# A mixture-of-experts loop: the planner's order against an order written out by hand

## The chip, the cores and the metric

The kernel runs on one core of one Trainium2 chip. The metric is the device time of one execution in microseconds (us), the median of several runs. The kernel is one launch; it moves 524 MB between the chip's main memory and the core's SBUF.

## The reference

A bidirectional encoder of two layers over 1024 tokens and 16 leading meta tokens, D = 1024. Each layer has an attention and a recurrent (RWKV-7) group of heads, an output projection and a LayerNorm, and then the part that this case is about, a mixture of 32 experts of which each token takes two:

```
def expert_block(args):
    xe, e = args
    return (jax.nn.silu(xe @ w1[e]) * (xe @ w3[e])) @ w2[e]
...
y = jnp.zeros((T, D)).at[row_tok].add(yb * row_gate[:, None])
...
h = _layer_norm(DN_ALPHA * h + ff, ln2_g[li], ln2_b[li])
```

w1 and w3 of an expert are 1024x256, w2 is 256x1024, so an expert has 3 MB of float32 weights, and a layer 96 MB. The 2080 choices of layer 0 (2048 of layer 1) spread over the experts, about 65 tokens each.

## The kernel before

`moe_layer` computes the experts one after the other with room for 96 tokens each (CAP); what is over goes through a general path, `tc.If(n_over > 0)`, that these inputs do not take. Products are float32 made from two parts: each operand is split into a high part (rounded to fp32r) and a low part (the remainder), and `mm3` issues three matmuls, high by high, high by low, low by high.

Per expert these steps run. A gather by row numbers (L1259, an indirect DMA issued on POOL) brings the tokens to `xs` (two buffers, one for even and one for odd experts). `turned` (L1229) transposes them on TensorE in two halves into the two PSUM buffers `tp`; ACT copies each half as high part `xT_hi` (L209), DVE subtracts to get `xT_lo` (L212). The weights come in three thirds of 1 MB, [128, 2048] each, by DMAs on the SP queue (L1211) into six buffers `raw`, so that two experts' weights fit; ACT makes the high part in four pieces (`w_hi`, L1216), and the low part is made by DVE in four pieces for the first two thirds, and by POOL in two pieces for the last third (`w_lo`, L1220). Six pairs of buffers hold the split thirds. 24 matmuls make the hidden layer `ph` (L201 to L203) from the first two thirds, one third for each half of `xT`. ACT takes tanh (L1239), DVE two instructions for the gated unit (L1240, L1241), TensorE transposes the result through `tp` (L1244), ACT and DVE split it (`aT`). 12 matmuls with the last third make `py`; ACT scales the left half to `y` (L1253), DVE the right half (L1254), and an indirect DMA on POOL scatters the rows to `y_rows` (L1255).

The program text has these steps expert by expert. The order on each engine's queue is set by the framework's planner, which runs a timing model over the whole program and takes what it expects to be ready; `tc.issue_after` pins only the first experts' splits behind the router. At run time each engine takes its queue in order and waits with semaphores. A buffer pool hands a new tile one of its free buffers, and the tile's first writer waits until the last reader of that buffer is done.

After the loop the check for the general path follows: six small DVE instructions on the counts (L1291 to L1299), a load of the result into a register of every engine (L1300), and a branch on every engine (L1302). Then `combine` (L334 to L354) takes both rows of each token from `y_rows` (`ys`), adds them on POOL (L344), forms `ALPHA * x + sum` with its row total on DVE (L346), and does the LayerNorm: a square with sum on ACT (L224), a power on POOL (L226), two passes on DVE (L227, L228). After layer 0 it transposes the rows for the next layer's projection; after layer 1 it stores the output. It works on 9 tiles of tokens after layer 0, on 8 after layer 1.

Of the kernel before, what the change touches and what calls it, by code (L numbers as in the profile page):

```python
# [11 lines left out]
F32 = mybir.dt.float32  # L12
# [22 lines left out]
NE = 32  # L35
# [135 lines left out]
def hybrid_encoder(ctx: ExitStack, tc: tile.TileContext, I, out):  # L171
# [141 lines left out]
    def combine(li, hT, pp):  # L313

        end = li == DEPTH - 1
        with ExitStack() as st:
# [20 lines left out]
            for i, n, col in tiles:  # L337
# [842 lines left out]
def moe_layer(tc, I, li, last, K, split, mm3, stack, rt, route, h1_rows, y_rows, nt, dram):  # L1180
# [18 lines left out]
    with pool(tc, name="mop", bufs=1, space=PSUM) as pp:  # L1199
# [5 lines left out]
        def weights(src, spaces=(ra, rc, rb), late=True):  # L1205

            r = []
            for q in range(3):
                raw = spaces[thirds[0] // 2 % len(spaces)].tile([128, 2048], F32, name="raw")
                thirds[0] += 1  # L1210
                nc.sync.dma_start(raw, src(q))  # L1211
                w = pair(ww, [128, 2048], "w")

                for c in range(4):
                    cs = slice(c * 512, (c + 1) * 512)
                    nc.scalar.activation(w.hi[:, cs], raw[:, cs], AF.Copy)  # L1216
# [4 lines left out]
                r.append(w)  # L1221
            return r

        def turned(x, n):
            xT = pair(wx, [128, 8, 128], "xT")[:, :, :n]
            for q in range(2):
                tp = pp.tile([128, 4, 128], F32, name="tp", bufs=2)
                for c in range(4):
                    nc.tensor.transpose(tp[:, c, :n], x[:n, (4 * q + c) * 128:(4 * q + c + 1) * 128], ident[:n, :n])  # L1229
                xT.last = split(xT[:, 4 * q:4 * q + 4], tp[:, :, :n])  # L1230
            return xT

        def expert(w, xT, n, vs, gs, rows):
            ph = pp.tile([128, 512], F32, name="ph", bufs=2)
            for kc in range(8):
                mm3(ph[:n], xT[:, kc], w[kc // 4][:, kc % 4 * 512:(kc % 4 + 1) * 512], start=kc == 0, stop=kc == 7)
# [4 lines left out]
            V.scalar_tensor_tensor(th, th, 0.5, ph[:n, 256:], op0=OP.mult, op1=OP.mult)  # L1241
            tp = pp.tile([128, 4, 128], F32, name="tp", bufs=2)
# [3 lines left out]
            split(aT, tp[:, 0:2, :n])  # L1246
            py = pp.tile([128, D], F32, name="py", bufs=2)
            for j in range(2):
                for c in range(2):
                    mm3(py[:n, j * 512:(j + 1) * 512], aT[:, c], w[2][:, c * D + j * 512:c * D + (j + 1) * 512],  # L1250
                        start=c == 0, stop=c == 1)
            y = wk.tile([128, D], F32, name="y")
            nc.scalar.activation(y[:n, :512], py[:n, :512], AF.Copy, scale=gs)  # L1253
            V.tensor_scalar(y[:n, 512:], py[:n, 512:], gs, None, op0=OP.mult)  # L1254
# [8 lines left out]
        def of(e, late=True):  # L1263
            return weights(lambda q: I["w_moe"][li, e, :, q * 2048:(q + 1) * 2048], late=late)

        def tokens(e):
            ins = gather(xs[e % 2][:CAP], h1_rows, XS[:CAP, e:e + 1], n_rows)
            return turned(xs[e % 2], CAP), ins
# [3 lines left out]


        (x0, _), (x1, second) = tokens(0), tokens(1)
        with tc.issue_after(route.act.ins), tc.issue_after(route.dve.ins), tc.issue_after(second.ins):
            ws = [of(0)]
        with tc.issue_after(x0.last[0].ins), tc.issue_after(x0.last[1].ins), tc.issue_after(second.ins):
            ws.append(of(1))
        xTs = [x0, x1]
        for e in range(NE):  # L1280
            if e + 1 < NE and e:
                ws.append(of(e + 1))
                xTs.append(tokens(e + 1)[0])
            expert(ws.pop(0), xTs.pop(0), CAP, VS[:CAP, e:e + 1], GS[:CAP, e:e + 1], views[e])


        tab = dram.tile([OVER * 128, 1], I32, name="ov_tab", tag="ov_tab", bufs=2)
        bex = dram.tile([1, OVER], I32, name="ov_bex", tag="ov_bex", bufs=2)
        gd = dram.tile([2 * n_rows, 1], F32, name=f"ov_gd{li}")
        nb = ov.tile([128, 4, NE], F32, name="nbs")  # L1290
        V.tensor_scalar(nb[:, 0], cnt, float(-CAP), 0.0, op0=OP.add, op1=OP.max)  # L1291
        ni = ov.tile([128, NE], I32, name="nis")
        V.tensor_scalar(ni, nb[:, 0], 127.0, None, op0=OP.add)
        V.tensor_scalar(ni, ni, 7, None, op0=OP.logical_shift_right)
        V.tensor_copy(nb[:, 0], ni)
        n1 = ov.tile([1, 1], F32, name="n1")
        V.tensor_reduce(n1, nb[0:1, 0], op=OP.add, axis=AX.X)
        nbi = ov.tile([1, 1], I32, name="nbi")
        V.tensor_copy(nbi, n1)  # L1299
        n_over = nc.values_load(nbi[0:1, 0:1], min_val=0, max_val=OVER,  # L1300
                                skip_runtime_bounds_check_because="2080 choices fill at most 21 such blocks")
        with tc.If(n_over > 0):  # L1302
            ini = ov.tile([128, OVER], I32, name="ini")
            V.tensor_copy(ini, bc(K("slot"), [128, OVER]))
            nc.sync.dma_start(tab.rearrange("(p b) o -> p (b o)", p=128), ini)
            for q, i in enumerate(route.order):
                n = META if i == NT else 128
                nc.sync.dma_start(gd[256 * i:256 * i + 2 * n].rearrange("(p j) o -> p j o", j=2), route.gates[:n, :, q, None])
            nc.gpsimd.memset(nb[:, 3], 1.0)
            V.tensor_tensor_scan(nb[:, 1], nb[:, 3], nb[:, 0], 0.0, op0=OP.mult, op1=OP.add)  # L1310
            V.tensor_tensor(nb[:, 2], nb[:, 1], nb[:, 0], op=OP.subtract)

            bx = ov.tile([1, OVER, NE], F32, name="bx")
            V.tensor_tensor(bx, bc(nb[0:1, 1:2, :], [1, OVER, NE]),
                            bc(K("iota32")[0:1, :OVER, None], [1, OVER, NE]), op=OP.is_le)
            bi = ov.tile([1, OVER], F32, name="bi")
            V.tensor_reduce(bi[:, :, None], bx, op=OP.add, axis=AX.X)
            V.tensor_scalar(bi, bi, float(NE - 1), None, op0=OP.min)
            bii = ov.tile([1, OVER], I32, name="bii")
            V.tensor_copy(bii, bi)  # L1320
            nc.sync.dma_start(bex[:], bii)
            tm = ov.tile([128, nt, NE], F32, name="otm")
            pos = ov.tile([128, nt], F32, name="pos")
            big = ov.tile([128, nt], F32, name="big")
            for j in range(2):
                V.tensor_tensor(tm, M[:, j], bc(nb[:, 2:3, :], [128, nt, NE]), op=OP.mult)
                V.tensor_reduce(pos, tm, op=OP.add, axis=AX.X)
                V.scalar_tensor_tensor(pos, pos, 128.0, rk[:, j], op0=OP.mult, op1=OP.add)
                V.tensor_scalar(big, rk[:, j], float(CAP), 1e5, op0=OP.is_lt, op1=OP.mult)
                V.scalar_tensor_tensor(pos, pos, float(-CAP), big, op0=OP.add, op1=OP.add)  # L1330
                pi = ov.tile([128, nt], I32, name="opi")
                V.tensor_scalar(pi, pos, 0.0, None, op0=OP.max)
                vv = ov.tile([128, nt], I32, name="ovv")
                for q, i in enumerate(route.order):
                    V.tensor_scalar(vv[:, q:q + 1], K("tokv")[:, 2 * i + j:2 * i + j + 1], -1.0, None, op0=OP.add)
                for i in range(nt):
                    nc.gpsimd.indirect_dma_start(out=tab[:], out_offset=bass.IndirectOffsetOnAxis(ap=pi[:, i:i + 1], axis=0),
                                                 in_=vv[:, i:i + 1], in_offset=None, bounds_check=OVER * 128 - 1,
                                                 oob_is_err=False)
            with tc.For_i(0, n_over, 1) as blk:  # L1340
                be = ov.tile([1, 1], I32, name="be", bufs=1)
                nc.sync.dma_start(be, bex[:, bass.ds(blk, 1)])
                ev = nc.values_load(be[0:1, 0:1], engines=[mybir.EngineType.SP], min_val=0, max_val=NE - 1,
# [340 lines left out]
```

## Time and profile before

| | before |
|---|---|
| median of 3 runs (lowest, highest) | 3257.91 us (3255.55, 3276.6) |
| the profiled execution: its time, its span | 3269.76 us, 3267.9 us |
| busy: PE, DVE, ACT, POOL | 2733.7, 2196.0, 1616.0, 1490.1 us |
| loop of layer 0, first weight split on DVE to last scatter | 1196.9 to 1579.7 us |
| loop of layer 1, the same | 2796.3 to 3195.9 us |
| gathers and scatters together (POOL's queue) | 33.84 MB in 128 DMAs |

The span is what lies between the first and the last instruction of that one execution. PE is TensorE; DVE, ACT and POOL are the vector, scalar and GpSimd engines. A stretch of the trace is given in us from the span's start.

### The profile page before, as it was taken

The numbers are of one execution on the slowest core, as the hardware profiler recorded it, in microseconds if no ns is written. First come the engines' busy times: TensorE is split into PE (matmuls) and PEld (weight loads), VectorE is DVE, ScalarE is ACT, GpSimd is POOL, SyncE is SP. The second block draws the span as 40 slices with busy tenths as digits, with TensorE's granted clock in tenths as the row PEclk, the third lists the DMA queues.
The fourth block names the chain that finished last, engine by engine and source line by source line (L and its number), as shares of the span: only waits on it lengthen the run. The fifth ranks groups of instructions, "written<-read, shape, count | busy, mean of one in ns | idle before, by whom it ended". The sixth has DMA issues, their size and how long they took to land. (4 is left out here: it accounts for less than half of the span.)

```text
span 3267.9 us, 58091 instructions
## 1 busy us (share of the span) xinstructions
PE 2733.7 (84%) x22160; PEld 2208.3 (68%) x22160; DVE 2196.0 (67%) x4048; ACT 1616.0 (49%) x3540; POOL 1490.1 (46%) x1194
## 2 busy tenths in 40 slices
PE   5989899979999978998388997898799889789780
PEld 5878687868777755665288866777687767456550
DVE  7667554566676687788656747446666676878865
ACT  5334454544445457776333435445344434677561
POOL 3665211143345437876555622112433544586664
PEclk9999899968888979999689988999787889799895
DMA  5345610233323459988614565102432326799774
GB/s 173 102 144 168 201 36 21 65 107 105 87 82 95 139 196 328 338 321 288 231 67 139 158 208 173 40 14 76 129 98 80 100 75 215 251 335 314 276 258 175
DMA packets 342732, 523.77 MB, mean 160 GB/s; under 512 B 110732, under 2 KB 263308, under 8 KB 315808
## 3 DMA queue, kind: packets, MB, share of 16 engines
q1 hardware_dynamic: 234832, 399.11, 37.7%
q10 hardware_dynamic: 93280, 87.04, 7.8%
q0 software_dynamic: 14336, 33.84, 3.2%
q8 instruction: 176, 2.88, 0.4%
q14 instruction: 108, 0.88, 0.1%
HBM read 406.57 MB, written 129.84 MB: 164 GB/s over the span
## 5 line engine op out<-in xcount | busy, mean ns | idle before, releaser
L1220 DVE TENSOR_TENSOR w_lo<-raw,w_hi 128x512 fp32r<-128x512 f32 x512 | 448.1, 932 | 12.8 <-ACT w_hi L1216 12.7
L1216 ACT ACTIVATE w_hi<-raw 128x512 fp32r<-128x512 f32 x768 | 419.8, 622 | 8.1 <-PE ph L203 8.1
L1220 POOL TENSOR_TENSOR w_lo<-raw,w_hi 128x1024 fp32r<-128x1024 f32 x128 | 314.7, 2480 | 39.0 <-ACT w_hi L1216 21.8
L201 PE MATMUL pj<-hT_hi,w_hi 128*128 128x352 f32 (+1 forms) x912 | 304.1, 334 | 3.7 <-ACT k L437 2.7
L202 PE MATMUL pj<-hT_lo,w_hi 128*128 128x352 f32 (+1 forms) x912 | 302.6, 332 | 0.6 <-DVE hT_lo L212 0.6
L203 PE MATMUL pj<-hT_hi,w_lo 128*128 128x352 f32 (+1 forms) x912 | 300.3, 330 | 0.0
L203 PE MATMUL ph<-w_hi,xT_lo 128*96 128x512 f32 x512 | 215.9, 422 | 22.0 <-DVE xT_lo L212 21.8
L201 PE MATMUL ph<-w_hi,xT_hi 128*96 128x512 f32 x512 | 217.2, 424 | 8.1 <-ACT xT_hi L209 7.9
L202 PE MATMUL ph<-w_lo,xT_hi 128*96 128x512 f32 x512 | 209.9, 410 | 0.4 <-DVE w_lo L1220 0.4
L1417 PE MATMUL e<-T,BK 64*128 64x128 f32 x1072 | 174.6, 342 | 36.6 <-ACT AA L1423 19.1
L1255 POOL DMA_INDIRECT y_rows<-y,VS x64 | 137.9, 2155 | 128.0 <-DVE y L1254 45.0
L212 DVE TENSOR_TENSOR pT_lo<-tr,pT_hi 128x512 fp32r<-128x512 f32 (+2 forms) x176 | 101.1, 592 | 128.6 <-ACT pT_hi L209 128.0
L201 PEld LDWEIGHTS pj<-hT_hi,w_hi 128*128 128x128 f32 x912 | 176.9, 194 | 14.2 <-issue 7.1
L1417 PEld LDWEIGHTS e<-T,BK 64*128 64x128 f32 x1072 | 147.1, 236 | 52.7 <-ACT AA L1423 21.9
L202 PEld LDWEIGHTS pj<-hT_lo,w_hi 128*128 128x128 f32 x912 | 176.9, 194 | 6.9 <-issue 5.2
L203 PEld LDWEIGHTS pj<-hT_hi,w_lo 128*128 128x128 f32 x912 | 176.7, 194 | 5.0 <-issue 4.3
L1562 POOL TENSOR_TENSOR sp<-ring,pc 64x256 f32<-64x256 f32 x126 | 84.9, 674 | 163.7 <-DVE ring L1575 149.7
L1422 DVE TENSOR_TENSOR T<-e,cc 64x512 f32<-64x512 f32 x134 | 92.1, 688 | 93.7 <-PE e L1417 89.6
L1429 POOL TENSOR_TENSOR AA<-AA,cc 128x256 f32<-128x256 f32 x67 | 52.0, 777 | 211.4 <-ACT AA L1423 150.9
L1259 POOL DMA_INDIRECT xs<-h_rows,XS x64 | 80.6, 1260 | 128.8 <-PE tp L1229 71.6
L209 ACT ACTIVATE pT_hi<-tr 128x512 fp32r<-128x512 f32 (+2 forms) x176 | 86.4, 516 | 94.1 <-PE tr L873 92.6
L201 PE MATMUL py<-w_hi,aT_hi 128*96 128x512 f32 x256 | 105.6, 413 | 31.7 <-ACT aT_hi L209 31.7
(423 smaller groups left out, 7874.3 us busy)
## 6 DMA issues: line engine op xcount, KB each, us to landing
raw<-in_w_moe_dram SPq DMA_DIRECT2D x192, 1024.0 KB
w_raw<-in_w_in_dram SPq DMA_DIRECT2D x38, 512.0 KB
T<-kr_d SPq DMA_DIRECT2D x134, 128.0 KB
ys<-y_rows SPq DMA_DIRECT2D x16, 1024.0 KB
a_d<-ht SPq DMA_DIRECT2D x25, 512.0 KB
h_rows<-h ACTq DMA_DIRECT2D x24, 512.0 KB
kr_d<-KR ACTq DMA_DIRECT2D x16, 576.0 KB
bk_d<-BK ACTq DMA_DIRECT2D x16, 576.0 KB
```

What stands on the lines that cost most here:

```text
L201: nc.tensor.matmul(o, a.hi, b.hi, start=start, stop=False)
L202: nc.tensor.matmul(o, a.hi, b.lo, start=False, stop=False)
L203: nc.tensor.matmul(o, a.lo, b.hi, start=False, stop=stop)
L209: hi = nc.scalar.activation(dst.hi, src, AF.Copy)
L212: return hi, e_lo.tensor_tensor(dst.lo, src, dst.hi.bitcast(F32), op=OP.subtract)
L1216: nc.scalar.activation(w.hi[:, cs], raw[:, cs], AF.Copy)
L1220: e.tensor_tensor(w.lo[:, cs], raw[:, cs], w.hi[:, cs].bitcast(F32), op=OP.subtract)
L1255: nc.gpsimd.indirect_dma_start(out=rows, out_offset=bass.IndirectOffsetOnAxis(ap=vs, axis=0), in_=y[:n], in_offset=None, bounds_check=2 * ...
L1259: return nc.gpsimd.indirect_dma_start(out=x, out_offset=None, in_=src[:], in_offset=bass.IndirectOffsetOnAxis(ap=xi, axis=0), bounds_check ...
L1417: nc.tensor.matmul(ps[o][:, u], BK[h, q0 + u].rearrange("p a t -> p (a t)"), T[h, q0 + u, o], start=True, stop=True)
L1422: V.tensor_tensor(T[b, q, o], ps[o][b], mask[b, None, :].to_broadcast([64, 4, 128]), op=OP.mult)
L1562: nc.gpsimd.tensor_tensor(sp[a], ring[a, :, o], pc[a, d, :, c:c + 1].to_broadcast([64, 4, 64]), op=OP.mult)
```

## The change

The loop over the experts gets an order written out for all engines (`tc.manual_schedule()`: each engine issues in the order of the program text). `expert` is taken apart into `hidden`, `gated`, `upright`, `product` and `stored`, and the loop's iteration e interleaves the second half of expert e with the first half of e+1 and the weight splits of e+2. All low parts are made on DVE, in four pieces each. Both halves of `y` are scaled on ACT. The check for the general path is made ahead of the loop, and its branch stands between the splits of expert 0's first two thirds and the loop; in the general path each third is now split as it is used, and the gathered rows go to a `raw` buffer instead of `xs`. In `combine` the POOL addition goes, and DVE does the sum in two passes. Shapes, buffers and their numbers stay.

```diff
-                nc.gpsimd.tensor_tensor(ys[:n, 0], ys[:n, 0], ys[:n, 1], op=OP.add)
+                nc.vector.scalar_tensor_tensor(x[:n], x[:n], ALPHA, ys[:n, 0], op0=OP.mult, op1=OP.add)
                 tot = wk.tile([128, 1], F32, name="tot")
-                nc.vector.scalar_tensor_tensor(x[:n], x[:n], ALPHA, ys[:n, 0], op0=OP.mult, op1=OP.add,
+                nc.vector.scalar_tensor_tensor(x[:n], x[:n], 1.0, ys[:n, 1], op0=OP.mult, op1=OP.add,
                                                accum_out=tot[:n])
...
-                e, k = (nc.gpsimd, 2 if late else 4) if q == 2 or not late else (V, 4)
-                for c in range(k):
-                    cs = slice(c * 2048 // k, (c + 1) * 2048 // k)
-                    e.tensor_tensor(w.lo[:, cs], raw[:, cs], w.hi[:, cs].bitcast(F32), op=OP.subtract)
+        def high(raw, w, c):
+            cs = slice(c * 512, (c + 1) * 512)
+            nc.scalar.activation(w.hi[:, cs], raw[:, cs], AF.Copy)
+
+        def low(raw, w, c):
+            cs = slice(c * 512, (c + 1) * 512)
+            V.tensor_tensor(w.lo[:, cs], raw[:, cs], w.hi[:, cs].bitcast(F32), op=OP.subtract)
+
+        def third(raw):
+            w = pair(ww, [128, 2048], "w")
+            for c in range(4):
+                high(raw, w, c)
+                low(raw, w, c)
+            return w
...
-            nc.scalar.activation(y[:n, :512], py[:n, :512], AF.Copy, scale=gs)
-            V.tensor_scalar(y[:n, 512:], py[:n, 512:], gs, None, op0=OP.mult)
+            for j in range(2):
+                nc.scalar.activation(y[:n, j * 512:(j + 1) * 512], py[:n, j * 512:(j + 1) * 512], AF.Copy, scale=gs)
...
+        raws = [of(0), of(1)]
+        tokens(0)
+        second = tokens(1)
+        nb, nbi, known = excess()
+
+        with tc.issue_after(route.act.ins), tc.issue_after(route.dve.ins), tc.issue_after(known.ins), tc.issue_after(second.ins):
+            ws = {0: [third(raws[0][q]) for q in range(2)]}
+        overflow(nb, nbi)
...
+        with tc.manual_schedule():
+            xTs[0] = turned(xs[0], CAP)
+            first(0, 0)
+            tokens(2)
+            first(0, 1)
+            tanh(0)
+            gate(0)
+            xTs[1] = turned(xs[1], CAP)
+            tokens(3)
+            portion(0, 2)
+            raws.append(of(2))
+            for q in range(3):
+                portion(1, q)
+            raws.append(of(3))
+            for e in range(NE):
+                more, new = e + 1 < NE, e + 2 < NE
+                aT = upright(ths.pop(e), CAP)
+                if more:
+                    first(e + 1, 0)
+                portion(e + 2, 0)
+                if more:
+                    first(e + 1, 1)
+                portion(e + 2, 1)
+                if new:
+                    raw, w = raws[e + 2][2], pair(ww, [128, 2048], "w")
+                    ws[e + 2].append(w)
+                    high(raw, w, 0)
+                if more:
+                    tanh(e + 1)
+                    gate(e + 1)
+                py = product(aT, ws.pop(e)[2], CAP)
+                if new:
+                    for c in range(4):
+                        if c:
+                            high(raw, w, c)
+                        low(raw, w, c)
+                    if e + 4 < NE:
+                        raws.append(of(e + 4))
+                stored(py, CAP, VS[:CAP, e:e + 1], GS[:CAP, e:e + 1], views[e])
+                if new:
+                    xTs[e + 2] = turned(xs[e % 2], CAP)
+                    if e + 4 < NE:
+                        tokens(e + 4)
```

In it `first(e, half)` issues the 12 matmuls of `hidden` for one half, `portion(e, q)` is `third` on expert e's third q, `of(e)` the three loads of expert e, `tokens(e)` its gather.

## Rows read from the trace of the kernel before

**Rows 1.** Stretches of the two loops: us, busy of PE, PEld, DVE, ACT, POOL (instructions), clock, DMA share, GB/s
```profile
1216.20:1375.90 159.70, 136.03 (x628) 89.44 (x627) 122.86 (x195) 113.09 (x234) 122.74 (x56) 0.97 0.94 323
1375.90:1571.80 195.90, 174.04 (x788) 118.51 (x786) 161.90 (x229) 134.73 (x276) 128.88 (x65) 0.95 0.83 293
...
2939.40:3186.10 246.70, 205.34 (x915) 138.24 (x914) 193.39 (x271) 159.96 (x328) 158.87 (x77) 0.93 0.81 283
```

**Rows 2.** Timeline, ACT: tanh of experts, start, us, [idle before <- releaser]
```profile
1216.22 0.37 ACT L1239 ACTIVATE th<-ph 96x256 f32<-96x256 f32 x1
1230.57 0.38 ACT L1239 ACTIVATE th<-ph 96x256 f32<-96x256 f32 x1 [9.82 <-PE ph L203]
...
1375.84 0.38 ACT L1239 ACTIVATE th<-ph 96x256 f32<-96x256 f32 x1 [1.82 <-PE ph L203]
...
1571.82 0.38 ACT L1239 ACTIVATE th<-ph 96x256 f32<-96x256 f32 x1 [4.07 <-PE ph L203]
...
2815.27 0.38 ACT L1239 ACTIVATE th<-ph 96x256 f32<-96x256 f32 x1 [0.33 <-PE ph L203]
...
3186.07 0.38 ACT L1239 ACTIVATE th<-ph 96x256 f32<-96x256 f32 x1 [2.47 <-PE ph L203]
```

**Rows 3.** Timeline, layer 0, late: DVE's queue and PE behind it
```profile
1533.09 4.58 DVE L1220 TENSOR_TENSOR w_lo<-raw,w_hi 128x512 fp32r<-128x512 f32 x4
...
1537.60 1.01 DVE L212 TENSOR_TENSOR xT_lo<-tp,xT_hi 128x384 fp32r<-128x384 f32 x2
1538.19 0.58 PE L1244 MATMUL tp<-cc,th 96*128 96x96 f32 x2 [1.80 <-DVE xT_lo L212]
```

**Rows 4.** Timeline, layer 1: pieces of one regular expert
```profile
3158.49 2.19 ACT L1216 ACTIVATE w_hi<-raw 128x512 fp32r<-128x512 f32 x4
...
3160.70 2.48 DVE L1220 TENSOR_TENSOR w_lo<-raw,w_hi 128x512 fp32r<-128x512 f32 x4
...
3165.25 0.39 PE L202 MATMUL ph<-w_lo,xT_hi 128*96 128x512 f32 x1
3165.48 0.40 PE L203 MATMUL ph<-w_hi,xT_lo 128*96 128x512 f32 x1
```

**Rows 5.** Groups by line and shape, 1240 to 1376 us: xcount | busy us, mean ns
```profile
L1220 DVE TENSOR_TENSOR w_lo<-raw,w_hi 128x512 fp32r<-128x512 f32 x96 | 70.1, 787 | 0.0
L1220 POOL TENSOR_TENSOR w_lo<-raw,w_hi 128x1024 fp32r<-128x1024 f32 x26 | 62.1, 2414 | 0.3
...
L212 DVE TENSOR_TENSOR xT_lo<-tp,xT_hi 128x384 fp32r<-128x384 f32 x26 | 14.3, 550 | 12.1 <-ACT xT_hi L209 12.1
...
L209 ACT ACTIVATE xT_hi<-tp 128x384 fp32r<-128x384 f32 x25 | 12.0, 482 | 11.2 <-PE tp L1229 11.2
...
L1253 ACT ACTIVATE y<-py,at 96x512 f32<-96x512 f32 x12 | 8.1, 671 | 0.0
```

**Rows 6.** Timeline, layer 0: the first transposes of the loop
```profile
1205.21 1.51 PE L1229 MATMUL tp<-cc,xs 96*128 96x96 f32 x8 [9.24 <-DMA xs<-h_rows,XS]
```

**Rows 7.** Stretch 3210 to 3215 us, columns as in the first group: loads alone
```profile
3210.00:3215.00 5.00, 0.00 (x0) 0.00 (x0) 3.03 (x6) 1.24 (x2) 3.08 (x2) 0.50 1.01 424
```

**Rows 8.** The branch's line on each engine's sequencer: ns min/median/max, first and last start
```profile
L1302 PEldq COMPARE_BRANCH  x2: 236/302/368, 1575.1 to 3191.1; - x2
...
L1302 POOLq INC_SWDGE_SEM  x2: 1464/2090/2717, 1585.1 to 3198.5; - x2
```

**Rows 9.** Groups by line and shape, 3200 to 3268 us (combine after layer 1)
```profile
L344 POOL TENSOR_TENSOR ys<-ys 128x1024 f32<-128x1024 f32 x8 | 23.4, 2944 | 10.5 <-DMA ys<-y_rows 10.5
L228 DVE SCALAR_TENSOR_TENSOR h<-hc,ln_st,l2b 128x1024 f32<-128x1024 f32 x8 | 16.4, 2055 | 0.9 <-POOL ln_st L226 0.9
L346 DVE SCALAR_TENSOR_TENSOR hc<-hc,ys 128x1024 f32<-128x1024 f32 x8 | 16.0, 2006 | 14.1 <-POOL ys L344 14.1
...
L227 DVE SCALAR_TENSOR_TENSOR hc<-hc,ln_st,l2g 128x1024 f32<-128x1024 f32 x8 | 12.2, 1526 | 0.0
```

**Rows 10.** Timeline, same stretch: a pass on DVE with POOL idle
```profile
3248.06 1.21 DVE L346 SCALAR_TENSOR_TENSOR hc<-hc,ys 128x1024 f32<-128x1024 f32 x1
```

More of the change, by code (lines that the diff above doesn't have):

```diff
@@ L1203, in moe_layer, with loaded @@
         thirds = [0]
-        def weights(src, spaces=(ra, rc, rb), late=True):
+        def loaded(src, spaces=(ra, rc, rb)):
             r = []
@@ L1211, in weights @@
                 nc.sync.dma_start(raw, src(q))
[L1212 to L1216, printed above, removed]
-                e, k = (nc.gpsimd, 2 if late else 4) if q == 2 or not late else (V, 4)
-                for c in range(k):
-                    cs = slice(c * 2048 // k, (c + 1) * 2048 // k)
-                    e.tensor_tensor(w.lo[:, cs], raw[:, cs], w.hi[:, cs].bitcast(F32), op=OP.subtract)
-                r.append(w)
-            return r
+                r.append(raw)
+            return r
+        def high(raw, w, c):
[10 more added lines that the diff above has]
+            return w
         def turned(x, n):
@@ L1229, in turned, with hidden, gated @@
                     nc.tensor.transpose(tp[:, c, :n], x[:n, (4 * q + c) * 128:(4 * q + c + 1) * 128], ident[:n, :n])
-                xT.last = split(xT[:, 4 * q:4 * q + 4], tp[:, :, :n])
+                split(xT[:, 4 * q:4 * q + 4], tp[:, :, :n])
             return xT
[L1233 to L1236, printed above, removed]
+        def hidden(ph, w, xT, n, half):
+            for kc in range(4):
+                mm3(ph[:n], xT[:, 4 * half + kc], w[:, kc * 512:(kc + 1) * 512], start=half == kc == 0,
+                    stop=half == 1 and kc == 3)
+        def gated(ph, n):
             th = wk.tile([128, 256], F32, name="th")[:n]
@@ L1241, in expert, with upright @@
             V.scalar_tensor_tensor(th, th, 0.5, ph[:n, 256:], op0=OP.mult, op1=OP.mult)
+            return th
+        def upright(th, n):
             tp = pp.tile([128, 4, 128], F32, name="tp", bufs=2)
@@ L1246, in expert, with product @@
             split(aT, tp[:, 0:2, :n])
+            return aT
+        def product(aT, w, n):
             py = pp.tile([128, D], F32, name="py", bufs=2)
@@ L1261, in gather, with of @@
                                                 bounds_check=rows - 1, oob_is_err=False)
-        def of(e, late=True):
-            return weights(lambda q: I["w_moe"][li, e, :, q * 2048:(q + 1) * 2048], late=late)
+        def of(e):
+            return loaded(lambda q: I["w_moe"][li, e, :, q * 2048:(q + 1) * 2048])
         def tokens(e):
-            ins = gather(xs[e % 2][:CAP], h1_rows, XS[:CAP, e:e + 1], n_rows)
-            return turned(xs[e % 2], CAP), ins
+            return gather(xs[e % 2][:CAP], h1_rows, XS[:CAP, e:e + 1], n_rows)
@@ L1271, in moe_layer @@
         views = dram_disjoint_views(y_rows[:], NE)
[L1274 to L1284, printed above, removed]
@@ L1295, in moe_layer @@
[L1295 to L1333, printed above, removed]
-                for q, i in enumerate(route.order):
[L1335 to L1343, printed above, removed]
-                                    skip_runtime_bounds_check_because="clamped above")
-                vs = ov.tile([128, 2], I32, name="ovs", bufs=1)
-                nc.sync.dma_start(vs[:, 0:1], tab[bass.ds(blk * 128, 128)])
-                V.tensor_scalar(vs[:, 1:2], vs[:, 0:1], 1, None, op0=OP.logical_shift_right)
-                gather(xs[0], h1_rows, vs[:, 1:2], n_rows)
-                gs = ov.tile([128, 1], F32, name="ogs", bufs=1)
-                nc.gpsimd.memset(gs, 0.0)
-                gather(gs, gd, vs[:, 0:1], 2 * n_rows)
-                w = weights(lambda q: I["w_moe"][li, bass.ds(ev, 1), :, q * 2048:(q + 1) * 2048]
-                            .rearrange("a p f -> p (a f)"), spaces=(ra if last else rc,))
-                expert(w, turned(xs[0], 128), 128, vs[:, 0:1], gs, y_rows[:])
@@ new lines, in excess @@
+        def excess():
+            nb = ov.tile([128, 4, NE], F32, name="nbs")
+            V.tensor_scalar(nb[:, 0], cnt, float(-CAP), 0.0, op0=OP.add, op1=OP.max)
+            ni = ov.tile([128, NE], I32, name="nis")
+            V.tensor_scalar(ni, nb[:, 0], 127.0, None, op0=OP.add)
+            V.tensor_scalar(ni, ni, 7, None, op0=OP.logical_shift_right)
+            V.tensor_copy(nb[:, 0], ni)
+            n1 = ov.tile([1, 1], F32, name="n1")
+            V.tensor_reduce(n1, nb[0:1, 0], op=OP.add, axis=AX.X)
+            nbi = ov.tile([1, 1], I32, name="nbi")
+            return nb, nbi, V.tensor_copy(nbi, n1)
@@ new lines, in moe_layer, with first @@
+        raws = [of(0), of(1)]
[5 more added lines that the diff above has]
+        overflow(nb, nbi)
+        phs, ths, xTs = {}, {}, {}
+        def first(e, half):
+            if half == 0:
+                phs[e] = pp.tile([128, 512], F32, name="ph", bufs=2)
+            hidden(phs[e], ws[e][half], xTs[e], CAP, half)
@@ new lines, in portion, with tanh, gate @@
+        def portion(e, q):
+            if e < NE:
+                ws.setdefault(e, []).append(third(raws[e][q]))
+        def tanh(e):
+            ths[e] = wk.tile([128, 256], F32, name="th")[:CAP]
+            nc.scalar.activation(ths[e], phs[e][:CAP, :256], AF.Tanh, scale=0.5)
+        def gate(e):
+            th, ph = ths[e], phs.pop(e)
+            V.scalar_tensor_tensor(th, th, 1.0, ph[:CAP, :256], op0=OP.add, op1=OP.mult)
+            V.scalar_tensor_tensor(th, th, 0.5, ph[:CAP, 256:], op0=OP.mult, op1=OP.mult)
@@ new lines, in moe_layer @@
+        with tc.manual_schedule():
[9 more added lines that the diff above has]
+            raws.append(of(2))
+            for q in range(3):
+                portion(1, q)
[29 more added lines that the diff above has]
+                        tokens(e + 4)
```

78 lines of the change are left out of this document (69 added, 9 removed).

## The prediction, made blind

> **What bounds the kernel now.** I looked first at the stretches of the two expert loops [rows 1]. No engine is full in any of them: PE is the busiest with 0.83 to 0.89 of the time, DVE has 0.77 to 0.83, and the second part of each loop is worse fed (283 and 293 GB/s at a DMA share of 0.81 and 0.83) than the first (323 GB/s). So the loop is bound by the order of hand-overs between engines. The pace is read from ACT's tanh, one for each expert [rows 2]: layer 0 takes (1571.82 - 1216.22) / 31 = 11.47 us an expert, layer 1 (3186.07 - 2815.27) / 31 = 11.96 us. Between 1230.57 and 1375.84 thirteen intervals lie, 11.17 us each; from 2939.40 to 3186.10 twenty, 12.34 us each. The planner's order fits in the first third of a loop and then no longer fits what the chip does. What that looks like stands in the timeline of a late expert [rows 3]: DVE makes four low parts in 4.58 us, POOL being at its own low part meanwhile, and only then the two `xT_lo`, on which PE's next transposes wait 1.80 us.
>
> **The terms of the loop.** Prices of single steps, all from regular stretches. Matmuls are issued 3165.48 - 3165.25 = 0.23 us apart and the last ends 0.17 us later [rows 4]. High parts in a run take 2.19 / 4 = 0.55 us each, low parts without POOL 2.48 / 4 = 0.62 us [rows 4]; beside POOL's low parts they take 0.787 us in the mean, and POOL needs 2.414 us for two pieces' worth, 1.21 us a piece [rows 5]. `xT_lo` takes 0.55, `xT_hi` 0.48, half a `y` on ACT 0.67 us [rows 5], of which the next instruction in a run waits some 0.6. Eight transposes take 1.51 us [rows 6], two then 0.38.
>
> One price is weighed against a rule. A low part on DVE costs 0.62 us where POOL takes 1.21 us and slows DVE's own besides [rows 4, 5]; by these rows DVE's low parts go from 8 x 0.787 = 6.3 us to 12 x 0.62 = 7.4 us an expert, and POOL's 4.8 us go. The Trainium skill (Perfetto Trace Analysis, Optimizing Scalar/DVE Operations) warns that GpSimd and DVE share an SBUF read port, so moving operations between those two might not help. By that warning I would count nothing for the moves to DVE, here and in `combine`, and the time would be 7 us longer than my forecast.
>
> With that no engine is full: DVE has 7.4 + 1.1 (`xT_lo`) + about 1.2 for `aT_lo` and the gate (an estimate) = 9.7 us an expert, ACT 12 x 0.55 + 2 x 0.48 + 2 x 0.6 + about 0.6 for tanh and `aT_hi` = 9.3 us, PE 36 x 0.23 + ten transposes = 10.2 us at most. The pace is then set by the chain that closes an iteration of the written order. I start where the 24 hidden matmuls of e+1 end. PE goes on with `product(e)`, 12 x 0.23 + 0.17 = 2.93 us. Tanh, the gate, the three remaining high parts (0.3 + 3 x 0.55 = 2.0 us) and the first half of `y` run on ACT and DVE beside it. When the product ends: second half of `y` 0.6, `xT_hi` of e+2 0.48, `xT_lo` 0.55 (until then the PSUM buffer `tp`, which `upright(e+1)` needs, is held), two transposes 0.38, and then the 24 hidden matmuls of e+2, 5.52 us. Sum 10.46, and five hand-overs from engine to engine, which no row prices; I take 0.05 us each, **10.7 us an expert**. The lower end is the chain with free hand-overs, 10.46, the upper one 11.17, what the planner's order reaches in its good part with hand-overs of the same kind.
>
> What queues behind what: on ACT the tanh of e+1 stands behind nine high parts of e+2, and each of these waits for its load, so a late load would hold the gate on DVE and PE's next transposes. The loads of e+4 are issued on SP behind the low parts of e+2 that free their buffers, two experts ahead; a gather, also two ahead, stands on POOL behind the scatter. Traffic per expert is 3 x 1.049 MB and twice 33.84 MB / 128 = 0.264 MB, 3.68 MB. At 323 GB/s for a share of 0.94 [rows 1], so 344 GB/s at a full share, that is 10.7 us: just covered. Loads alone reach 424 GB/s [rows 7], which would be 8.7 us, so some slack is likely. In the loop no wait of an engine on a weight load is seen now.
>
> Start: the written order puts tanh 0 ahead of expert 0's last third and expert 1's three, so ACT has 16 high parts after it, 8.8 us, then `xT_hi`, `aT_hi` and nine more, some 6 us: tanh 1 comes about 15 us after tanh 0, and 14.35 us lie there now [rows 2]. I count the start at 5 us over the pace in each layer. The branch ahead of the loop is hidden by PE's wait for the first gather, 9.24 us [rows 6]: by then DVE has its eight low parts done (5 us) and a branch takes 0.3 us [rows 8]. If the cover were gone it would cost its register load and branch, under 1 us, and POOL's balancing of DMA counts, up to 2.7 us [rows 8], or, with the loads of expert 2 queued behind it, up to 10 us a layer. At the end of the loop the branch now lies beside the wait for the last scatter, so nothing is won there.
>
> Sum of the loops: layer 0 31 x (11.47 - 10.7) - 5 = 19 us, layer 1 31 x (11.96 - 10.7) - 5 = 34 us, **53 us** less.
>
> **Combine.** After layer 1 DVE's passes take 2.06 and 2.01 us in the mean because POOL's addition of 2.94 us runs beside them [rows 9]; undisturbed such a pass takes 1.21 us [rows 10], I take 1.25. Eight tiles now cost 16.4 + 16.0 = 32.4 us there; after, 8 x 3 x 1.25 = 30 us, and `hc` at L227 loses 12.2 - 8 x 1.25, 2 us, of the same disturbance. The first tile has a pass of 1.25 us in place of the addition. That is 5 us. After layer 0 DVE also has the low parts of `hT` and POOL the next weights' low parts, so I take 2 us, with -3 to +6 as ends. Together **7 us**.
>
> The six small instructions of the check are the same and already stand ahead of the loop in the trace. `turned`, the scatter and the gather are the same instructions in another place.
>
> **Rivals.**
> - *Slower: the pair of buffers for the last third is held by the product* (0.07). Iteration e takes its pair for third 3 of e+2 before `product(e)` is issued. At that point four of six pairs hold something, two are free, the older one since the first half of `first(e+1)`. If the pool instead gave it the pair that `product(e)` reads, ACT's first high part would wait for the product, and tanh e+1 stands behind it. The chain would be 2.93 + 0.55 + 0.3 + 1.65 + 1.2 + 0.48 + 0.55 + 0.38 + 5.52 + 0.25 = 13.8 us an expert: 31 x 2.33 + 31 x 1.84 + 10 - 7 = 132 us more, **3390**. It decides from the point where this chain exceeds 11.7 us. Other ways to be slower by more than 1%, a stall by the planner around the fixed block above all, get 0.04.
> - *Hand-overs and the clock eat it* (0.18). The irregular stretches show a granted clock of 0.93 and 0.95, a mean over time at 2.4 and at 1.2 GHz [rows 1]. At 0.95 the 36 matmuls cost 8.28 / 0.95 - 8.28 = 0.44 us more, and hand-overs of 0.1 us 0.25: 11.4 us an expert, 62 x 0.7 = 43 us above the forecast, **3241**. Against it: the regular first part of layer 0 has 0.97 with PE no busier than it will be.
> - *The loads set the pace* (0.13). If 323 GB/s is all that the mix of loads and row transfers gives, 3.68 MB take 11.4 us, and this becomes the rival above; if 344, 10.7 us and the forecast. In between, at 11.04 us, **3219**. For it speaks a DMA share of 0.94, against it that no engine waits for a weight load and the 424 GB/s [rows 7]. The Trainium skill (SBUF — State Buffer, SBUF: two separate sides) gives about 358 GB/s between main memory and a core; as an estimate from that figure an expert would take 10.3 us and loads would not set the pace.
>
> **How the numbers follow.** Against the profiled execution of 3269.76 us, 53 + 7 = 60 us less gives 3210; that execution lies 11.85 us above the median of the three, so for the median 3257.9 - 60 = **3198 us**. The forecast has 0.58. Its own range: the pace from 10.46 to 11.17 us (-15 to +29), the starts 0 to +10, `combine` -4 to +7: 3179 to 3240. To leave out no more than 2 in 10 it goes up to within the second rival and somewhat past it, 3262, and down to 3172 for a pace that loads and hand-overs help; the slower rival and what lies past these ends stay out. A change of 1% is 33 us, about what a measurement of this kernel can tell from none. Faster by more (under 3225): forecast 0.58 and most of the loads' rival, 0.70; within 1%: 0.19; slower: 0.11.
>
> **What would show it.** Of the profile after: tanh to tanh 10.4 to 10.9 us all through both loops, with no growth after the first third; DVE's low parts at 0.62 to 0.7 us in the mean and none on POOL; PE's longest wait, under 1 us, ahead of `upright` for `xT_lo`; both loops of equal length, about 362 us from the first split to the last scatter; DVE's passes in the last `combine` at 1.25 us each. Wrong would be: high parts on ACT waiting for `py` matmuls (the slower rival), high parts waiting for a load of `raw` (loads), a clock under 0.95 in the loop, or weight loads of expert 2 issued more than 15 us after the first gather (the branch).

## The result, and the profile after

The kernel after takes 3244.98 us (median of 20 runs, 3223.72 to 3262.36), the one before 3273.77 us in the same session: a ratio of 0.992, 95% interval 0.990 to 0.9941, 19 to 33 us less. The forecast had 60 us less. The profiled execution after has a span of 3242.1 us, 25.8 less than before. I cut both profiles, and those of three experiments below, at the same events:

```
us between events                       before  e1      e6      e9      after
start to last routing step, layer 0     1196.8  1192.9  1174.6  1200.3  1188.8
from there to the first tanh              19.4    20.3    15.2    17.5    16.7
first tanh to last (31 experts)          355.6   356.5   365.2   365.8   365.9
last tanh to layer 1's projections       391.9   381.6   387.6   396.1   378.1
from there to last routing step, 1       832.5   831.5   848.5   837.4   837.8
from there to the first tanh              19.1    19.2    16.0    16.6    16.3
first tanh to last, layer 1              370.8   366.9   371.5   371.2   371.5
last tanh to the end                      81.8    74.7    75.7    72.6    67.1
```

(e1 has the new `combine` alone, e6 is the change without it, e9 the change with the branch behind the loop. The fourth row ends where ACT reads the last of layer 1's projections, L437.) The first and the fifth row are stages that the change doesn't touch. In layer 0 no engine's order of instructions differs there, and still they end between 1174.6 and 1200.3 us: whole profiles can't be compared to better than some 20 us. The short rows are steadier; what the long ones say is checked below by the medians of several runs. **The loops did not get faster.** Layer 0's is 10 us longer, layer 1's the same. All of the gain lies around them: 14 us at the end of each layer, 3 at the start of each.

The stretches of the loop after, columns as in [rows 1]:

```profile
1205.50:1376.00 170.50, 143.06 (x644) 100.16 (x643) 142.31 (x255) 132.75 (x267) 28.04 (x27) 0.92 0.90 315
1376.00:1571.40 195.40, 167.23 (x773) 117.86 (x772) 155.00 (x277) 145.86 (x294) 30.45 (x32) 0.94 0.87 301
...
2937.60:3175.00 237.40, 204.25 (x921) 142.58 (x920) 185.90 (x333) 174.67 (x351) 36.17 (x38) 0.93 0.85 299
```

The granted clock is lower than before in the first part (0.92 against 0.97). Cut at each tanh, the loop shows only two kinds of expert behind its first two:

```profile
1244.65:1257.22 12.57, 10.91 (x47) 7.61 (x46) 9.79 (x18) 8.97 (x19) 1.91 (x2) 0.86 0.94 323
1257.22:1268.21 10.99, 9.33 (x47) 6.66 (x46) 9.26 (x17) 8.96 (x18) 1.91 (x2) 1.00 0.86 302
1268.21:1280.78 12.57, 10.91 (x47) 7.61 (x46) 9.79 (x18) 8.97 (x19) 1.91 (x2) 0.86 0.95 344
1280.78:1291.77 10.99, 9.33 (x47) 6.65 (x46) 9.27 (x17) 8.97 (x18) 1.91 (x2) 1.00 0.79 283
```

Both kinds do the same work with 47 matmuls. One takes 10.99 us at a clock of 1.00, the other 12.57 us at 0.86. In layer 1 they take 11.10 and 12.64 us. Of the 29 periods behind the first two, twelve are long in layer 0 and fourteen in layer 1. The timeline of one long expert shows how it comes about (start, us, [idle before <- releaser]; ACT, DVE and PE together):

```profile
1270.54 0.39 PE L203 MATMUL py<-w_hi,aT_lo 128*96 128x512 f32 x1
1270.77 0.82 PE L1235 MATMUL tp<-cc,xs 96*128 96x96 f32 x8
1270.97 1.26 ACT L1272 ACTIVATE y<-py,at 96x512 f32<-96x512 f32 x2 [0.82 <-PE py L203]
1272.13 0.86 ACT L209 ACTIVATE xT_hi<-tp 128x384 fp32r<-128x384 f32 x2
...
1272.64 1.02 DVE L212 TENSOR_TENSOR xT_lo<-tp,xT_hi 128x384 fp32r<-128x384 f32 x2 [0.74 <-ACT xT_hi L209]
...
1273.25 0.39 PE L1256 MATMUL tp<-cc,th 96*128 96x96 f32 x2 [1.66 <-DVE xT_lo L212]
...
1273.42 0.46 PE L201 MATMUL ph<-w_hi,xT_hi 128*96 128x512 f32 x1
...
1275.15 0.63 PE L203 MATMUL ph<-w_hi,xT_lo 128*96 128x512 f32 x1
1275.58 0.63 PE L201 MATMUL ph<-w_hi,xT_hi 128*96 128x512 f32 x1
...
1279.66 0.39 PE L203 MATMUL ph<-w_hi,xT_lo 128*96 128x512 f32 x1
1279.89 0.39 PE L201 MATMUL ph<-w_hi,xT_hi 128*96 128x512 f32 x1
```

ACT has nothing to do for 0.82 us until the whole product is there, then makes both halves of `y`, and only then `xT_hi`. PE waits 1.66 us for `xT_lo`. This wait is in each of the 58 periods behind the first two. In the long ones the matmuls start 0.43 us apart for a while after it (1275.58 - 1275.15), at 1.2 GHz, and then 0.23 us again, at 2.4 GHz. Seven or eight of them at 0.2 us more are the 1.6 us. In all 26 long experts of both layers the first slow matmul starts 0.2 to 1.3 us behind the start of `upright` (L1256), and the last one at most 4.2 us behind it.

The prices of single steps are as forecast. DVE's low parts, and the passes of the last `combine` by line and shape, which answer to [rows 9]:

```profile
L1221 DVE TENSOR_TENSOR w_lo<-raw,w_hi 128x512 fp32r<-128x512 f32 x143 | 88.1, 684 | 1.9 <-ACT w_hi L1217 1.9
```
```profile
L227 DVE SCALAR_TENSOR_TENSOR hc<-hc,ln_st,l2g 128x1024 f32<-128x1024 f32 x8 | 10.2, 1275 | 0.0
L228 DVE SCALAR_TENSOR_TENSOR h<-hc,ln_st,l2b 128x1024 f32<-128x1024 f32 x8 | 10.1, 1277 | 0.4 <-POOL ln_st L226 0.4
L344 DVE SCALAR_TENSOR_TENSOR hc<-hc,ys 128x1024 f32<-128x1024 f32 x8 | 9.7, 1219 | 12.8 <-DMA ys<-y_rows 12.8
L346 DVE SCALAR_TENSOR_TENSOR hc<-hc,ys 128x1024 f32<-128x1024 f32 x8 | 9.7, 1218 | 0.0
```

### The profile page after: what moved, and what is told of

Its sections match the earlier page's. It is cut to its first block, busy times and chain, and to the rows that moved or that the text cites. A ratio compares the mean times of both kernels' runs of the same rounds, so it can differ in the third digit from the quotient of the medians.

```text
span 3242.1 us, 57910 instructions
## 1 busy us (share of the span) xinstructions
PE 2737.0 (84%) x22160; PEld 2231.9 (69%) x22160; DVE 2174.9 (67%) x4257; ACT 1658.0 (51%) x3604; POOL 1040.8 (32%) x1049
## 5 line engine op out<-in xcount | busy, mean ns | idle before, releaser
L1221 DVE TENSOR_TENSOR w_lo<-raw,w_hi 128x512 fp32r<-128x512 f32 x768 | 472.8, 684 | 9.3 <-ACT w_hi L1217 9.1
L1217 ACT ACTIVATE w_hi<-raw 128x512 fp32r<-128x512 f32 x768 | 412.1, 620 | 0.0
L1273 POOL DMA_INDIRECT y_rows<-y,VS x64 | 64.5, 1007 | 617.6 <-ACT y L1272 595.7
L201 PE MATMUL ph<-w_hi,xT_hi 128*96 128x512 f32 x512 | 226.9, 443 | 3.4 <-ACT w_hi L1217 3.4
L202 PE MATMUL ph<-w_lo,xT_hi 128*96 128x512 f32 x512 | 222.7, 435 | 1.3 <-DVE w_lo L1221 1.3
L1551 DVE TENSOR_TENSOR sb<-sb,dg 128x16 f32<-128x16 f32 (+8 forms) x270 | 107.1, 397 | 40.5 <-POOL dg L1543 33.4
L203 PEld LDWEIGHTS ph<-w_hi,xT_lo 128*96 128x96 f32 x512 | 93.1, 182 | 43.1 <-issue 3.2
L201 PEld LDWEIGHTS ph<-w_hi,xT_hi 128*96 128x96 f32 x512 | 93.4, 182 | 42.5 <-ACT w_hi L1217 4.1
L202 PEld LDWEIGHTS ph<-w_lo,xT_hi 128*96 128x96 f32 x512 | 93.1, 182 | 40.2 <-DVE w_lo L1221 2.3
```

The lines of the kernel that those rows point to most:

```text
L201: nc.tensor.matmul(o, a.hi, b.hi, start=start, stop=False)
L202: nc.tensor.matmul(o, a.hi, b.lo, start=False, stop=False)
L203: nc.tensor.matmul(o, a.lo, b.hi, start=False, stop=stop)
L1221: V.tensor_tensor(w.lo[:, cs], raw[:, cs], w.hi[:, cs].bitcast(F32), op=OP.subtract)
L1273: nc.gpsimd.indirect_dma_start(out=rows, out_offset=bass.IndirectOffsetOnAxis(ap=vs, axis=0), in_=y[:n], in_offset=None, bounds_check=2 * ...
L1551: V.tensor_tensor(sb[:, :, cs], sb[:, :, cs], dg[:, :, t_:t_ + 1].to_broadcast([128, n, w]), op=OP.mult)
```

## Experiments

My theory after the trace: PE's one idle stretch per expert, 1.66 us, makes the clock fall in every second or third expert. The rivals: loads set the pace, or the clock falls whatever PE does. Ratios are to the kernel before.

**PE kept busy in the stretch, nothing else moved (e2).** After `turned(e + 2)`:

```
+ phs[e + 2] = pp.tile([128, 512], F32, name="ph", bufs=2)
+ for c in range(4):
+     nc.tensor.matmul(phs[e + 2][:CAP], xTs[e + 1].hi[:, c], ws[e + 1][2].hi[:, c * 512:...], start=True, stop=True)
```

> The changed kernel with four useless matmuls of 128x512 (0.23 us each at the full clock, 0.92 us) put on PE between the turned transposes and the upright ones, where PE idles 1.66 us in each expert; they write into the accumulator of a later expert, which that expert's first matmul overwrites, so nothing of the result is changed, and no real work is moved. Theory (the idle stretch makes the granted clock fall to 0.86 in every second or third expert, which is the whole difference between the periods of 12.57 and 10.99 us): with the idle stretch cut to about 0.7 us the clock stays at 1.00, all periods are about 11.0 us, layer 0's loop falls from 365.9 to about 341 us and layer 1's from 371.5 to about 343 us: about 3190 us, ratio to before 0.973 to 0.977. Rival 1 (loads set the pace: 3.7 MB per expert at 310 to 340 GB/s are 10.9 to 11.9 us): the periods stay at a mean of 11.5 or more, within 15 us of the changed kernel. Rival 2 (the clock falls whatever PE does in the gap, as the chain alone sets it): periods of 12.57 us remain, no difference, or slower by the matmuls.

Measured 3203.06 us, ratio 0.9793 (0.9751 to 0.9835). All periods but the first two are 10.98 to 10.99 us in layer 0 and 11.10 in layer 1; the loops take 347.9 and 351.2 us, 18 and 20 less than after. A stretch of 100 us of it:

```profile
1300.00:1400.00 100.00, 93.47 (x462) 65.42 (x461) 86.86 (x156) 81.30 (x164) 17.11 (x18) 1.00 0.97 341
```
```profile
1302.79 0.39 PE L1256 MATMUL tp<-cc,th 96*128 96x96 f32 x2 [0.72 <-DVE xT_lo L212]
```

So useless work on PE makes the kernel 1.3% faster. The chain is as long as it was; only the clock has changed. Both rivals fall. The median is 13 us above the theory's 3190, and the loops are where they lie: 7 and 8 us longer than the 341 and 343 expected, because the first two periods take some 29 us together and layer 1's others 11.10.

**`y` behind `xT_hi` on ACT (e3).** The block with `turned` and `tokens` stands ahead of `stored`:

```
+ if new:
+     xTs[e + 2] = turned(xs[e % 2], CAP)
  ...
  stored(py, CAP, VS[:CAP, e:e + 1], GS[:CAP, e:e + 1], views[e])
- if new:
-     xTs[e + 2] = turned(xs[e % 2], CAP)
```

> The changed kernel with one step moved: the outputs y of an expert (two evictions of 0.63 us on ACT) come behind the turned transposes and their xT_hi on ACT, not ahead of them. Theory (PE's 1.66 us of waiting for xT_lo is the 1.26 us of y on ACT plus the hand-overs): the wait falls to 0.3 to 0.6 us, the clock stays at 0.97 or more, the period is 9.8 to 10.7 us by whichever comes last of PE's 9.33 us, DVE's 9.3 to 9.8 us and the loads; 34 to 60 us less in each loop, 3125 to 3180 us, ratio to before 0.955 to 0.972. Rival (loads or DVE set the pace already, PE's wait only moves to another place): mean period 11.3 us or more, less than 20 us from the changed kernel, ratio above 0.986.

Measured 3152.66 us, 0.9636 (0.9593 to 0.9679). Periods 10.18 to 10.30 us, loops 324.3 and 326.3 us. PE still waits, 0.85 to 0.93 us where 0.3 to 0.6 were expected, and the DMA is nearly full:

```profile
1307.58 0.39 PE L1256 MATMUL tp<-cc,th 96*128 96x96 f32 x2 [0.93 <-DVE xT_lo L212]
```
```profile
1300.00:1400.00 100.00, 91.14 (x453) 64.92 (x452) 92.11 (x168) 86.27 (x176) 18.05 (x19) 1.00 0.99 363
```

Still it is PE's chain that sets this pace: 9.33 us of work and 0.93 of waiting make 10.26, and no engine waits for a load. A DMA share of 0.99 alone does not show a limit.

**The prediction's own chain (e5).** The accumulator in two tiles, so that the first half of `y` runs beside the product, as the forecast had assumed:

```
- py = pp.tile([128, D], F32, name="py", bufs=2)
+ py = [pp.tile([128, 512], F32, name="py", bufs=4) for j in range(2)]
```

> The changed kernel with the product's accumulator as two tiles of 128x512 in place of one of 128x1024, so that the first half of y need not wait for the second half's matmuls; order and arithmetic unchanged. It is the assumption of the prediction's chain (first half of y beside the product, 0.6 us behind it instead of 1.16). Theory (in the trace after, ACT idles 0.82 us for the whole product, and both halves of y then lie in PE's idle stretch of 1.66 us): the stretch falls to about 1.1 us, the period to about 10.4 us, and the clock stays at 1.00 as it does with a wait of 1.16 us in the regular part of the kernel before; loops 40 to 47 us shorter each, 3150 to 3175 us, ratio to before 0.963 to 0.971. Rival (an idle stretch of 1.1 us still lets the clock fall in every second expert): mean 11.2 us, about 3200 us, ratio 0.978. Rival (the loads hold it at 11): 3190 us.

Measured 3181.83 us, 0.9726 (0.9693 to 0.976). The periods are 10.42 us in layer 0 and 10.53 in layer 1, with the starts 10.65 and 10.75 in the mean; the wait is 1.08 us, and the clock stays:

```profile
1300.90 0.39 PE L1256 MATMUL tp<-cc,th 96*128 96x96 f32 x2 [1.08 <-DVE xT_lo L212]
```
```profile
1300.00:1400.00 100.00, 89.38 (x439) 63.69 (x440) 91.28 (x164) 86.25 (x174) 19.01 (x20) 1.00 0.99 355
```

The period is the theory's. The loops, 330.3 and 333.4 us, are 36 and 38 us shorter than after, where the theory had 40 to 47, and the median is 7 us above its range. At a DMA share of 0.99 no engine waits for a load here either.

**The turned transposes one expert earlier, ahead of the product (e4).**

```
+ if e + 3 < NE:
+     xTs[e + 3] = turned(xs[(e + 1) % 2], CAP)
+     if e + 5 < NE:
+         tokens(e + 5)
  py = product(aT, ws.pop(e)[2], CAP)
```

> The changed kernel with the turned transposes of an expert made one expert earlier (those of e+3 in the step of e) and put ahead of the product, so that xT_hi and xT_lo are made beside the product and PE has no idle stretch left between its instructions; the gathers go the same step earlier. Theory: PE's work of 9.33 us per expert runs without a wait, the clock stays at 1.00, and the next limit shows: DVE at 9.3 to 9.8 us busy or the loads (3.7 MB at 344 GB/s are 10.7 us, at the 424 GB/s of rows 7 8.7 us); period 9.8 to 10.7 us, 3120 to 3175 us, ratio to before 0.953 to 0.970, and the same as with y moved, or a little less. Rival (the loads set the pace of 11.8 already): within 20 us of the changed kernel, and PE waits as long as before, only for w_hi or w_lo.

Measured 3149.35 us, 0.9637 (0.9594 to 0.9679), no better than e3. Its third and fourth period are 9.12 and 9.13 us, PE's work without a gap; then they spread from 8.3 to 12.4, and ACT waits for loads, which no engine does in the loops of before, after, e3 or e5 (layer 0's loop: us in total, times, longest):

```profile
ACT w_hi L1217 <- DMA raw<-in_w_moe_dram: 27.9, 28, 2.1
```

**Half of each load left out of e4 (e7).** `nc.sync.dma_start(raw[:, :1024], src(q)[:, :1024])`, and the parts read that half twice.

> The kernel with the turned transposes one expert earlier, with half of every weight load left out (the first 1024 of 2048 columns are loaded and used twice), all work on the engines unchanged; the values computed are others. Theory (with the idle stretch gone the loads set the pace of 10.4 us at a DMA share of 0.98 to 1.01 and 360 GB/s): the period falls to the 9.12 us of that kernel's first experts, 9.1 to 9.4 us in both loops, clock 1.00, about 3070 to 3090 us, ratio to before 0.939 to 0.946. Rival (DVE, busy 9.1 of 10.3 us, and ACT with their hand-overs set the 10.4 us): within 15 us of 3149 us, ratio 0.959 to 0.964.

Measured 3100.33 us, 0.9474 (0.9442 to 0.9507). The periods are 9.1 to 9.23 us but for the first two and the last, as expected. The loops take 295.1 and 296.6 us, 26 us less each than in e4; I had reckoned with 34, as if the first period of 20 us could shrink too, so the median is 10 us above the range. PE is at last full:

```profile
1300.00:1400.00 100.00, 100.00 (x503) 71.25 (x502) 99.62 (x187) 95.20 (x197) 85.65 (x23) 1.00 0.74 233
```

So behind the idle stretch stand the loads: in e4, 360 GB/s at a DMA share of 0.99 (1245 to 1500 us), which for 3.68 MB are 10.2 us an expert. That is why e4 gains nothing over e3. The Trainium skill (SBUF — State Buffer, SBUF: two separate sides) gives about 358 GB/s between main memory and a core; e4 agrees with it, shorter stretches reach more [rows 7].

**Splitting started earlier (e8).** In e4, the last third of expert 0 and all of expert 1 are split ahead of the first tanh, where ACT idles:

```
+ portion(0, 2)
+ raws.append(of(2))
+ portion(1, 0)
  xTs[0] = turned(xs[0], CAP)
  ...
  first(0, 1)
+ portion(1, 1)
+ portion(1, 2)
+ raws.append(of(3))
  tanh(0)
```

> The kernel with the turned transposes one expert earlier, with the high and low parts of expert 0's last third and of expert 1's three thirds moved ahead of the first tanh, where ACT idles 6.6 and 7.3 us and the DMA share is 0.07 to 0.5, so that the raw buffers come free and the loads of expert 2 begin some 10 to 15 us earlier. Theory (the loads set the pace from there to the end of the loop): each loop ends 8 to 15 us earlier, 3120 to 3135 us, ratio to before 0.954 to 0.959. Rival (the start is hidden, as the pace later is set by engines): no difference, 3149 us. Rival on the other side (the high parts wait on ACT for a load that has not landed, and the first xT_hi behind them): the first tanh comes later by more than 3 us, slower by up to 6 us.

Measured 3132.78 us, 0.9561 (0.9526 to 0.9596): the best version that does the whole work, some 110 us under after by the medians. The second tanh follows the first after 11.1 us instead of 20.4, and the loops take 312.9 and 313.1 us (e4: 321.1 and 322.3). The first tanh comes 1 to 2 us later, the other side's point, but is paid back.

**`combine` alone, on the kernel before (e1), and undone in the kernel after (e6).** The edit is that of the diff at L341 to L346.

> The kernel before with one edit of the change alone: in the combine both passes (ALPHA times the row plus one half of ys, then the other half with the row sum) on DVE and none on POOL; the expert loops are as before. Theory (the loops gave nothing, the stages around them gave it all): the profiles of before and after differ by 13.4 us between the last tanh of layer 0 and the last projection of layer 1's input, and by 14.8 us between the last tanh of layer 1 and the end, so this kernel is 20 to 28 us faster than before, about 3245 to 3254 against 3274, ratio 0.991 to 0.994. Rival (the combine gives the 7 us of the prediction, and the other 19 us come from the loops' starts, 10.7 and 11.7 us earlier): 5 to 9 us faster, ratio 0.997 to 0.9985.

> The changed kernel with one edit of the change undone: POOL adds the two halves of ys again in the combine, and DVE makes one pass less. Theory (the combine on DVE is worth 13 us by the runs of the kernel that had this edit alone, 18 by its profile): 10 to 18 us slower than the changed kernel, ratio to before 0.995 to 0.9985; the loops have the same periods of 10.99 and 12.57 us. Prediction: 7 us, ratio 0.994. Rival (it is worth the 28 us by which the stages around the loops differ between the profiles of before and after): 28 us slower, ratio 1.000 to 1.001.

Measured: e1 3257.06 us, 0.9959 (0.9936 to 0.9983); e6 3257.91 us, 0.9959 (0.9937 to 0.9981). Added alone it takes 13 us away, undone it gives 13 back. Each has a wide interval (e1: 6 to 21 us), so the forecast's 7 is too little but not far outside, and my first theory, 20 to 28 us, too much. By the table it is 10 us after layer 0 and 7 to 9 after layer 1, together some 4 us more than the medians say.

**The branch behind the loop again (e9).** The call `overflow(nb, nbi)` stands after the last expert.

> The changed kernel with one part undone: the check for the general path (the branch) stands behind the expert loop again, with the six small instructions of the count left ahead of it. Theory (the branch at the loop's end was not hidden by the last scatter: from the last scatter to the first load of ys 8.1 and 6.4 us lie before, 4.5 and 3.6 us after, and the loads of ys follow each other more slowly): 3 to 4 us longer at the end of each loop, 5 to 10 us in all, ratio to before 0.9935 to 0.995, and the start of the loop as in the changed kernel (16.3 to 16.7 us from the last routing instruction to the first tanh). Rival (the prediction: both places are hidden): no difference in those two stretches, ratio 0.992. Rival (the branch ahead of the loop costs something too): the first tanh comes over 1 us sooner after the routing.

Measured 3266.21 us, 0.9979 (0.9958 to 0.9999), 0.6% or 19 us slower than after (by the intervals some 10 to 29), about twice what I expected. The start doesn't change (17.5 and 16.6 us to the first tanh). The end of layer 0 does. SP's queue, first the kernel after, then e9:

```profile
1545.68 19.73 SPq L334 DMA_DIRECT2D hc<-h_rows  x8
1565.45 0.43 SPq L334 DMA_DIRECT2D hm<-h_rows  x1
1574.12 0.35 SPq L216 DMA_DIRECT2D l2g<-in_ln_g_dram  x1
1574.51 0.43 SPq L216 DMA_DIRECT2D l2b<-in_ln_b_dram  x1
1578.75 0.89 SPq L414 DMA_DIRECT2D w_raw<-in_w_in_dram  x2
1584.84 1.47 SPq L339 DMA_DIRECT2D ys<-y_rows  x3
```
```profile
1597.92 3.91 SPq L334 DMA_DIRECT2D hc<-h_rows  x8
1601.88 0.76 SPq L334 DMA_DIRECT2D hm<-h_rows  x1
1602.93 0.31 SPq L339 DMA_DIRECT2D ys<-y_rows  x1
1604.83 0.35 SPq L216 DMA_DIRECT2D l2g<-in_ln_g_dram  x1
1606.03 0.35 SPq L216 DMA_DIRECT2D l2b<-in_ln_b_dram  x1
1607.32 1.49 SPq L339 DMA_DIRECT2D ys<-y_rows  x2
```

The last scatter is issued at 1580.3 us in after and 1592.6 in e9. With the branch there, the rows `hc` and the norm's constants are loaded only behind it, ahead of and beside `ys`; without it they are long there. The first pass of the `combine` starts 7 us after the last scatter in after and 21 us in e9. What the loads wait for is not SP's own branch. The branch's line on two sequencers of e9 (ns min/median/max, first and last start):

```profile
L1309 SPq COMPARE_BRANCH  x2: 50/50/50, 1553.7 to 3197.8; - x2
L1309 POOLq INC_SWDGE_SEM  x2: 1456/2086/2717, 1596.3 to 3217.4; - x2
```

SP was past its branch at 1553.7 us. Its first `hc` load then waited until 1597.7, the moment at which POOL's balancing of DMA counts at the branch ends (1596.3 + 1.46), and POOL starts that only when the last scatter has landed. The profile itself puts this wait down to a gather that had landed long before, so the link is read from the times. Part of the cost is the planner's placing: in the kernel before some of the `hc` loads stood ahead of the branch, so there it cost less: before and e6 differ by 4 us after layer 0 and by 6 after layer 1.

## Why the prediction was wrong

**The step that failed: the first half of `y` runs beside the product.** The chain had 0.6 us for the second half alone. One accumulator tile holds both halves, and ACT waited until all its matmuls were done, so `y` cost 1.16 us there. From the product's first matmul to `upright` (1268.01 to 1273.25) the chain took 5.24 us where 4.56 had been worked out without hand-overs; the two transposes took 0.17 instead of 0.38 us ([rows 6] lies in a stretch at the lower clock), and the period came to 10.99 us instead of 10.46 to 10.7. With the accumulator in two tiles it is 10.42 (e5), so this step costs 0.57 us an expert, 18 us a loop (e2 against e5).

**The second half of the error: what the wait does to the clock.** The stretch had been set at "under 1 us"; it is 1.66, and twelve and fourteen experts lose 1.6 us to it: 18 and 20 us (e2). Behind the first two periods the mean pace was 11.65 and 11.85 us instead of 10.7. The second rival had this effect and nearly this time (11.4 us, 3241) and 0.18. That its time is so near is luck: it had the loops 10 us shorter and the rest 7, and the loops became 11 us longer. What I set against it was the clock of 0.97 in the first part of the loop before, with PE as busy. That mean hides two levels: up to 1240 us the clock is 0.78, and the regular part behind it has 1.00, with waits of PE of 1.08 us at a time.

```profile
1240.00:1376.00 136.00, 121.43 (x570) 80.09 (x569) 102.81 (x171) 101.55 (x209) 112.01 (x51) 1.00 0.97 327
```

The sign of what a longer wait does stood in the same trace. Behind the wait of 1.80 us in [rows 3] the matmuls start 0.43 us apart:

```profile
1539.00 0.63 PE L201 MATMUL ph<-w_hi,xT_hi 128*96 128x512 f32 x1
1539.43 0.63 PE L202 MATMUL ph<-w_lo,xT_hi 128*96 128x512 f32 x1
```

From 1364 us to the end of layer 0's loop PE has seven waits of 1.8 to 2.4 us, and six of them are followed by such matmuls. Of the written orders, e5, e3 and e2 with 1.08, 0.93 and 0.72 us keep 1.00 too, and the loops of after, e6 and e9, with 1.66, lose it. Why it does so in some experts and not in each isn't settled.

**Loads.** No load was late at 11 us an expert, as forecast; the rival's 11.04 did not come. But the limit is near: 10.2 us at 360 GB/s. The 424 GB/s of [rows 7] were no measure for the loop.

**The slower rival** did not come: no high part waits for a product.

**Starts.** 14.36 + 13.79 us for the first two periods, 6.7 over twice the forecast pace, where 5 were counted. That tanh 0 itself would come 3 us sooner after the routing I had not seen; e9 shows that it isn't the branch, e6 that it isn't the `combine`. Which part of the fixed order does it was not tried.

**Combine.** After layer 1 the sizes of the passes are right: 29.5 us for three passes over eight tiles against 30, and 2 us less at L227; yet the stage became 7 to 9 us shorter, where these sizes gave 5. After layer 0 I had 2 us and it is 10: DVE's passes there had been slowed just as much by POOL (3.36 us for one at L228 before, 1.28 after). The warning of the Trainium skill (Perfetto Trace Analysis, Optimizing Scalar/DVE Operations) that moving work between GpSimd and DVE might not help did not come true here: e1 and e6 show 13 us.

**The branch.** "Nothing is won there" was wrong: I looked at the last scatter and not at the loads on SP that wait for POOL's part of the branch. [rows 8] had that part. In the trace before it ends at 1586.6 and 3201.2 us, and the first loads of `ys` start just behind it:

```profile
1586.88 0.31 SPq L339 DMA_DIRECT2D ys<-y_rows  x1
3201.39 0.34 SPq L339 DMA_DIRECT2D ys<-y_rows  x1
```

Against the kernel before the move gave up to 4 and 6 us.

**The range.** Added up, its own upper ends (29, 10 and 7 us) give 3244 and not 3240. The measured 3245 lies below the upper end of 3262, but not for the reason given there: the loops, by which the range was drawn, gave nothing.

Summed by stretches: starts -6, loops +11, end of layer 0 -14, end of layer 1 -15, the untouched stages -3: -26 us. The forecast's -60 had -53 in the loops and -7 in `combine`. With the step that it had assumed put in (e5) the loops reach what was forecast: 330.3 and 333.4 us against 31 x 10.7 + 5 = 337.

## What to carry to other kernels

In an order written by hand, work out the wait that is left on PE in each round, and read the granted clock round by round: a mean of 0.93 was a mixture of rounds at 1.00 and at 0.86. An eviction waits for the whole accumulator tile, so split the tile where the first half should leave early. Of a branch that is moved, follow the loads that wait for it, on every queue, not only the engines. A DMA share near 1 is a limit only where something waits for a load.

## What the runs showed of the hardware

A wait of PE of 1.66 us per expert went with a fall to 1.2 GHz for seven or eight matmuls in 26 of the 58 periods behind the first two, each time right behind that wait, and with four more matmuls in its place (e2, wait 0.72 us) in none. Without the fall everything in the loop repeats to 0.01 us (e2: 10.98 or 10.99 in layer 0), so the steps can be read from one expert.
